# Masks by replaced scores, earlier direct down weights and a split last bank in a hybrid decoder block

## The chip, the cores and the metric

The kernel runs on one core of a Trainium2 chip. The metric is the device time of one execution in microseconds (us), the median of several runs. TensorE (PE) does the matrix products and its weight loads (PEld), VectorE (DVE), ScalarE (ACT) and GpSimd (POOL) the work on elements, SyncE (SP) issues nearly all transfers.

## The reference, cut to what matters

One decoder block on x of 512 x 1024 (float32): an RMS norm, one input projection, a mixture of dilated windows (8 heads), a sparse attention in which an indexer picks at most 128 keys for each query, a gated merge, and a SwiGLU FFN of width 2816 with a final RMS norm. The two pieces that the change touches:

```python
# sparse attention: the 128 best keys of each query
score = jnp.einsum('bqh,bqhs->bqs', wi_blk, jax.nn.relu(dots)) * IDX_SCALE
score = jnp.where(causal[None], score, -jnp.inf)
_, sel = lax.top_k(score, topk)
valid = sel <= q_pos[None, :, None]
...
# the end of the block
x = x + (jax.nn.silu(h @ w_gate) * (h @ w_up)) @ w_down
return rmsnorm(x, norm_final)
```

## The kernel before

All matrices are float32. Each operand of a product is split into a rounded high part and a low rest (`hi`, `lo`), and `mm3` (L202) makes each product with three matmuls. Weights come by SP into `raw` buffers (five), ACT writes `whi`, and DVE or POOL subtracts to get `wlo` (L159 to L175); `PLO` sets which of the two does it. The FFN's down projection is done in two parts: 18 of the 22 blocks of 128 rows through a scheme with seven products instead of eight, the last four (`LAST = 4`) directly.

PE's order over the middle of the program is the order in which the code is traced. The other engines' orders are set by a scheduler that places operations by priority levels: attention at level 2, the filling projections at level 3, the top-k at level 4, so that top-k operations fall between others on DVE. Each engine runs its own list strictly in order. A bank of `acc` (three of them hold the projections), of `tr` (two) or `s` (three) is used again only when its reader is done.

**The top-k** (`topk_ops`, L626). Blocks 3, 2 and 1 of 128 queries have 512, 384 and 256 keys. Sixteen rounds of `max` (the eight largest of a row) and, but for the last round, `match_replace` (those eight are overwritten with `LOWEST` in `cur`) leave 128 values in `top`. Then six operations for each block make the mask: the count of values equal to the 128th (`e0`, L642), the positions equal to it (`eq`, L644), their running count (L646), the equal ones that are still wanted (L647), plus the greater ones (L648), and 0 or -1e30 (L649). Keys after the query hold `LOWEST` from an affine select (L872).

**What stands around it.** While the masks are made, PE runs attention steps of the first mixer (`sc`, `pT`, `y`) between projections: `proj`, four products with 256 columns for the values of the first mixer, block of queries by block; then `slot`, the queries of the second. `va_parts` (L554) empties each `proj` bank by two ACT copies (L564) and two DVE subtractions (L565). `rope_T` (L487) copies a finished `slot` (L490), has SP move its rows crosswise into `sw` (L493), and multiplies and adds on DVE (`straight` L497, `crossed` L500 and L501).

**The end.** With `pair` at its last value, PE makes the remaining products of the seven-product scheme; then DVE adds what these leave to `x1` (ten operations, at L1157, L1159, L1167, L1168 and L1170). The eight direct weights (`W`, L1171) are traced behind these sums: POOL makes the `wlo` of each h = 0, DVE that of each h = 1. Then for each block b of 128 tokens and each half h of 512 columns PE makes 12 matmuls into `po[b, h]`, DVE adds (L1184), ACT squares with a row sum (L1187), POOL multiplies by the norm weights `gF` (L1188), DVE adds up the mean square `v` (L1190). `rstd_of` (L257) is a square root on ACT, a reciprocal and two steps of refinement on DVE (L265 and L269, twice). At last DVE scales h = 0 (L1193), ACT h = 1 (L1195), and SP issues both stores.

Of the kernel before, what the change touches and what calls it, by code (L numbers as in the profile page):

```python
# [11 lines left out]
F32 = mybir.dt.float32  # L12
F32R = mybir.dt.float32r
AF = mybir.ActivationFunctionType
ALU = mybir.AluOpType

P = 128
T = 512
D = 1024
KT = D // P  # L20
NB = T // P
# [3 lines left out]
NF = DFF // P  # L25
D_IN = 4808
TOPK = 128
EPS = 1e-6
NEG = -1.0e30
LOWEST = -3.0e38  # L30
ATTN_SCALE = HD ** -0.5
IDX_SCALE = (64 ** -0.5) * (8 ** -0.5)

# [5 lines left out]
def hybrid_block(ctx: ExitStack, tc: tile.TileContext, x, norm_mix, w_in, w_up_a, w_up_b, w_out,  # L39
                 norm_ffn, w_gate, w_up, w_down, norm_final, c_rope, c_ropeT, c_mask, out):  # L40
    nc = tc.nc
    x2 = x.rearrange("b t d -> (b t) d")
    out2 = out.rearrange("b t d -> (b t) d")
    win, wua, wub, wo = w_in[0], w_up_a[0], w_up_b[0], w_out[0]
    wg, wu, wd = w_gate[0], w_up[0], w_down[0]
# [3 lines left out]
    small = ctx.enter_context(tc.tile_pool(name="small", bufs=4))  # L49
    at_stack = ExitStack()  # L50
    wp = ctx.enter_context(tc.tile_pool(name="wp", bufs=1))
    ap = at_stack.enter_context(tc.tile_pool(name="ap", bufs=1))
# [160 lines left out]
    def trp(name="tr"):  # L213
        return ps.tile([P, 512], F32, tag="tr", bufs=2, name=name)
# [409 lines left out]
    top, cur = {}, {}  # L624

    def topk_ops():  # L626

        for r in range(TOPK // 8):
            for b in (3, 2, 1):
                src = score[b] if r == 0 else cur[b]  # L630
                yield nc.vector.max(top[b][:, 8 * r:8 * r + 8], src[:, :(b + 1) * P])
            if r < TOPK // 8 - 1:
                for b in (3, 2, 1):
                    w = (b + 1) * P
                    src = score[b] if r == 0 else cur[b]
                    yield nc.vector.match_replace(cur[b][:, :w], top[b][:, 8 * r:8 * r + 8], src[:, :w], LOWEST)
        for b in (3, 2, 1):
            w = (b + 1) * P
            thr = top[b][:, TOPK - 1:TOPK]
            need = small.tile([P, 1], F32, name="need")  # L640
            e0 = ap.tile([P, TOPK], F32, tag="e0", bufs=1, name="e0")
            yield nc.vector.tensor_scalar(e0, top[b], thr, None, op0=ALU.is_equal, op1=ALU.add, accum_out=need)  # L642
            eq = ap.tile([P, 512], F32, tag="eq", bufs=1, name="eq")[:, :w]
            yield nc.vector.tensor_scalar(eq, score[b][:, :w], thr, None, op0=ALU.is_equal)  # L644
            cs = cur[b][:, :w]
            yield nc.vector.tensor_tensor_scan(cs, eq, eq, 0.0, op0=ALU.add, op1=ALU.bypass)  # L646
            yield nc.vector.scalar_tensor_tensor(eq, cs, need, eq, op0=ALU.is_le, op1=ALU.mult)  # L647
            yield nc.vector.scalar_tensor_tensor(eq, score[b][:, :w], thr, eq, op0=ALU.is_gt, op1=ALU.add)  # L648
            yield nc.vector.tensor_scalar(score[b][:, :w], eq, 1.0, -NEG, op0=ALU.subtract, op1=ALU.mult)  # L649
            maskb[b] = score[b]  # L650

    topk = []
# [201 lines left out]
    score = {}  # L854
    for b in (3, 2, 1):
        w = (b + 1) * P
        score[b] = sc = ap.tile([P, 512], F32, tag="score", bufs=3, name=f"score{b}")
        sp = k2(name="scorep") if PH[0] >= 0 else None
        for hp in range(4):
            for s, p_ in enumerate(qk_units([(idxT[1 + hp], idxT[0], s, b) for s in range(2)], "dots")):  # L860
                h = 2 * hp + s
                rl = ap.tile([P, 512], F32, tag="sm", bufs=4, name="relu")
                nc.scalar.activation(rl[:, :w], p_[:, :w], AF.Relu)
                eng, to = (nc.gpsimd, sp) if h in PH else (nc.vector, sc)
                if h == 0 or h == PH[0]:
                    eng.tensor_scalar(to[:, :w], rl[:, :w], wis[:, b, h:h + 1], 1.0, op0=ALU.mult, op1=ALU.mult)
                else:
                    eng.scalar_tensor_tensor(to[:, :w], rl[:, :w], wis[:, b, h:h + 1], to[:, :w], op0=ALU.mult, op1=ALU.add)
                if sp is not None and h == NH - 1:
                    nc.vector.tensor_tensor(sc[:, :w], sc[:, :w], sp[:, :w], op=ALU.add)  # L870
            fill(DOTF)
        nc.gpsimd.affine_select(out=sc[:, b * P:w], in_=sc[:, b * P:w], compare_op=ALU.is_ge, fill=LOWEST, base=0,  # L872
                                pattern=[[-1, P]], channel_multiplier=1)
    drain()
    for b in (3, 2, 1):
# [76 lines left out]
    x1 = [load_x(b) for b in range(NB)]  # L952
# [26 lines left out]
    fp = ctx.enter_context(tc.tile_pool(name="fp", bufs=1))  # L979
# [5 lines left out]
    for h in range(2):  # L985
        W = chunk(wo, [(512 * h, 512)], per=1)
        po = [alloc("x1") for alloc in ((sps, sps, sps, trp) if h == 0 else (trp, sps, sps, sps))]
# [13 lines left out]
        for b in range(NB):  # L1001
            jk = k2(name="junk")
# [3 lines left out]
    gF = fp.tile([P, D], F32, name="gF")  # L1006
# [23 lines left out]
    for f in range(0, NF, 2):  # L1030
        G = []
        pair = f // 2
        W = chunk(wg, [(f * P, 256)])
        for j in range(2):
            p_ = acc("g")
            for k in range(KT):
                mm3(p_, (W[k][0][:, j * P:(j + 1) * P], W[k][1][:, j * P:(j + 1) * P]), h2[k], k == 0, k == KT - 1)
            g = fp.tile([P, 512], F32, tag="g", bufs=2, name="g")
# [3 lines left out]
        W = chunk(wu, [(f * P, 256)])  # L1042

        ops = fp.tile([P, 8, 256], F32, tag="ops", bufs=1, name="ops") if pair < NS else None
        for j in range(2):
            p_ = acc("u")
# [10 lines left out]
            tag, bufs = (("y", YB) if i >= 2 else ("rp", 2) if i == 1 else ("k2", K2))  # L1057
# [17 lines left out]
    po = {(b, h): banks[2 * b + h](f"o{b}{h}") for b in range(NB) for h in range(2)}  # L1075
# [19 lines left out]
    def product(b0, h, a, o, w, start, stop):  # L1095

        for i in range(2):
            c = slice(o + i * P, o + (i + 1) * P)
            mm3(po[b0 + i, h], (a[0][:, c], a[1][:, c]), w, start, stop)
# [45 lines left out]
    for pair in range(NS):  # L1145
        bring_back(pair + BACK)
        a, s5 = back[pair]
        w21, w22, u3 = second_weights(pair) if pair else first_of_second
        if pair == NS - 1:
            product(2, 0, a, 256, u3, False, True)  # L1150
        product(0, 0, a, 0, w21, pair == 0, False)
        product(0, 1, s5, 0, w22, pair == 0, False)
        if pair < NS - 1:
            product(2, 0, a, 256, u3, pair == 0, False)
    for i in range(2):
        o = x1[2 + i][1]
        nc.vector.tensor_tensor(o, o, po[2 + i, 0], op=ALU.subtract)  # L1157
        o = x1[2 + i][0]
        nc.vector.tensor_tensor(o, po[2 + i, 0], o, op=ALU.add)  # L1159
# [5 lines left out]
    for i in range(2):  # L1165
        o = x1[2 + i][0]
        nc.vector.tensor_tensor(o, po[2 + i, 1], o, op=ALU.add)  # L1167
        nc.vector.tensor_tensor(o, o, V[i], op=ALU.add)  # L1168
        o = x1[2 + i][1]
        nc.vector.tensor_tensor(o, o, c5[i], op=ALU.add)  # L1170
    W = {}  # L1171
    for f in range(NF - LAST, NF):
        for h in range(2):
            W[f, h] = chunk(wd[f * P:(f + 1) * P], [(512 * h, 512)], kts=1, per=1)[0]
    for i in range(2):
        nc.gpsimd.tensor_scalar(gF[:, i * 512:(i + 1) * 512], gF[:, i * 512:(i + 1) * 512], 0.0625, 1.0, op0=ALU.mult, op1=ALU.mult)
    for b in range(NB):
        v = None
        for h in range(2):
            for f in range(NF - LAST, NF):  # L1180
                mm3(po[b, h], (act[f][0][:, b * P:(b + 1) * P], act[f][1][:, b * P:(b + 1) * P]), W[f, h],
                    b >= 2 and f == NF - LAST, f == NF - 1)
            o = x1[b][h]
            nc.vector.tensor_tensor(o, po[b, h], o, op=ALU.add)  # L1184
            ss = small.tile([P, 1], F32, name="ss3")
            jk = fp.tile([P, 512], F32, tag="g", bufs=2, name="jk")
            nc.scalar.activation(jk, o, AF.Square, accum_out=ss)  # L1187
            nc.gpsimd.tensor_tensor(o, o, gF[:, h * 512:(h + 1) * 512], op=ALU.mult)  # L1188
            v2 = small.tile([P, 1], F32, name="v3")
            nc.vector.tensor_scalar(v2, ss, 1.0 / D, EPS if v is None else v, op0=ALU.mult, op1=ALU.add)  # L1190
            v = v2
        rs3 = rstd_of(v, 1, f"rs3_{b}", scaled=True)
        nc.vector.tensor_scalar(x1[b][0], x1[b][0], rs3, None, op0=ALU.mult)  # L1193
        nc.sync.dma_start(out2[b * P:(b + 1) * P, 0:512], x1[b][0])
        nc.scalar.activation(x1[b][1], x1[b][1], AF.Copy, scale=rs3)  # L1195
        nc.sync.dma_start(out2[b * P:(b + 1) * P, 512:1024], x1[b][1])


def _constants():
# [10 lines left out]
    n[d < 0] = 0  # L1210
    mask = np.where(n > 0, np.log(np.maximum(n, 1)) / ATTN_SCALE, NEG).astype(np.float32)
    return tab, tabT, mask
# [24 lines left out]
```

## Time and profile before

| what | us |
|---|---|
| median of 3 runs | 767.15 |
| lowest and highest run | 764.58, 769.06 |
| the profiled execution | 764.99 |
| its span, first to last instruction | 763.2 |
| PE busy in it | 733.3 |
| DVE, ACT, POOL busy | 503.4, 378.4, 258.8 |

An engine that is busy here is not always what the others wait for: a list of waits tells who waited for whom, a timeline tells when. The timeline gives start, duration, engine, line, output and inputs; in brackets is the idle time just before, and what ended it. Durations of neighbours overlap a little, since an engine takes up the next operation while the last one drains.

### The profile page before, as it was taken

To read this page: it belongs to the slowest core of one execution; us is meant where nothing else is said; L and a number is where in the kernel's file an instruction comes from. 1 tells how busy PE (TensorE), PEld (TensorE's weight loads), DVE (VectorE), ACT (ScalarE), POOL (GpSimd) and SP (SyncE) were. 2 spreads that over 40 slices of the span, in tenths; PEclk is the share of its full clock that TensorE was granted. 3 is DMA by queue.
4 is the path that set the end of the run, shared out by engine and by line. 5 is a ranking of instruction groups with operands and counts; after the bars stand their busy time and mean duration, and the time that the engine had idled before them with its cause. 6 is when DMAs were issued, how large, how long until landed. Compare 5 with 4: busy or idle time off the path is not lost.

```text
span 763.2 us, 10914 instructions
## 1 busy us (share of the span) xinstructions
PE 733.3 (96%) x3567; PEld 616.1 (81%) x3567; DVE 503.4 (66%) x1063; ACT 378.4 (50%) x771; POOL 258.8 (34%) x245
## 2 busy tenths in 40 slices
PE   8987998997999999999999999999999999999995
PEld 7976887886888888888887888888888888888874
DVE  5879998999757557848225444344454457877885
ACT  6366656665656666634246333333333334545553
POOL 1653567563554554523222222222222220000043
PEclk9999999999999999999999999999999999999999
DMA  7342243322342212443332343334433452756722
GB/s 266 96 124 70 67 120 91 95 65 70 84 126 70 69 57 69 141 137 105 100 85 69 103 131 110 104 105 131 131 105 104 130 179 84 230 171 212 248 84 110
DMA packets 76280, 88.70 MB, mean 116 GB/s; under 512 B 6256, under 2 KB 57600, under 8 KB 76224
## 3 DMA queue, kind: packets, MB, share of 16 engines
q1 hardware_dynamic: 76224, 88.02, 38.3%
q8 instruction: 28, 0.46, 0.2%
q14 instruction: 28, 0.23, 0.1%
HBM read 79.08 MB, written 5.64 MB: 111 GB/s over the span
## 4 chain that ended last, share of the span: by engine, by line
PE 79%; DVE 13%; ACT 3%; issue 3%; DMA 1%; POOL 1%; SPq 0%; DVEq 0%; ACTq 0%; POOLq 0%
PE u L204 5%; PE u L205 5%; PE u L203 5%; PE g L205 5%; PE g L204 5%; PE g L203 5%; PE o L205 4%; PE o L203 4%; PE o L204 4%; PE gate L203 3%; PE gate L204 3%; PE gate L205 3%; PE x L203 2%; PE x L205 2%; PE x L204 2%
## 5 line engine op out<-in xcount | busy, mean ns | idle before, releaser
L166 POOL TENSOR_TENSOR wlo<-raw,whi 128x512 fp32r<-128x512 f32 (+1 forms) x138 | 183.4, 1339 | 401.8 <-ACT whi L174 398.5
L174 ACT ACTIVATE whi<-raw 128x512 fp32r<-128x512 f32 (+1 forms) x206 | 126.7, 624 | 164.2 <-PE u L205 70.0
L166 DVE TENSOR_TENSOR wlo<-raw,whi 128x512 fp32r<-128x512 f32 x68 | 50.7, 746 | 67.6 <-ACT whi L174 67.1
L205 PE MATMUL g<-h2l,whi 128*128 128x512 f32 x176 | 68.7, 390 | 0.0
L203 PE MATMUL g<-h2h,whi 128*128 128x512 f32 x176 | 68.7, 390 | 0.0
L204 PE MATMUL g<-h2h,wlo 128*128 128x512 f32 x176 | 68.6, 390 | 0.0
L203 PE MATMUL u<-h2h,whi 128*128 128x512 f32 x176 | 68.5, 389 | 0.0
L204 PE MATMUL u<-h2h,wlo 128*128 128x512 f32 x176 | 68.5, 389 | 0.0
L205 PE MATMUL u<-h2l,whi 128*128 128x512 f32 x176 | 68.5, 389 | 0.0
L686 POOL TENSOR_SCALAR sm<-sm,st 128x256 f32<-128x256 f32 (+3 forms) x64 | 40.0, 632 | 60.1 <-DVE st L685 50.8
L203 PE MATMUL gate<-hTh,whi 128*128 128x512 f32 x128 | 51.6, 403 | 0.0
L205 PE MATMUL gate<-hTl,whi 128*128 128x512 f32 x128 | 50.2, 392 | 0.0
L204 PE MATMUL gate<-hTh,wlo 128*128 128x512 f32 x128 | 50.1, 392 | 0.0
L1050 DVE TENSOR_TENSOR u<-u,rb 128x512 f32<-128x512 f32 x22 | 15.2, 691 | 49.0 <-PE u L205 49.0
L681 ACT ACTIVATE sm<-sm,st 128x256 f32<-128x256 f32 (+3 forms) x64 | 35.6, 557 | 23.6 <-DVE st L680 23.5
L203 PE MATMUL slot<-hTh,whi 128*128 128x512 f32 x104 | 42.4, 407 | 1.8 <-DVE va L565 1.1
L203 PE MATMUL proj<-whi,hTh 128*128 128x256 f32 (+1 forms) x128 | 38.3, 301 | 3.7 <-DVE va L565 1.6
L205 PE MATMUL slot<-hTl,whi 128*128 128x512 f32 x104 | 41.6, 400 | 0.0
L204 PE MATMUL slot<-hTh,wlo 128*128 128x512 f32 x104 | 41.4, 398 | 0.0
L203 PEld LDWEIGHTS u<-h2h,whi 128*128 128x128 f32 x176 | 33.0, 188 | 6.9
L204 PEld LDWEIGHTS u<-h2h,wlo 128*128 128x128 f32 x176 | 33.0, 188 | 6.9
L204 PE MATMUL proj<-whi,hTl 128*128 128x256 f32 (+1 forms) x128 | 38.0, 297 | 0.6 <-DVE hTl L315 0.6
(351 smaller groups left out, 1849.1 us busy)
## 6 DMA issues: line engine op xcount, KB each, us to landing
raw<-in_w_in SPq DMA_DIRECT2D x54, 256.0 KB, 3.0
raw<-in_w_gate SPq DMA_DIRECT2D x44, 256.0 KB, 2.8
raw<-in_w_up SPq DMA_DIRECT2D x44, 256.0 KB, 2.9
raw<-in_w_down SPq DMA_DIRECT2D x43, 256.0 KB, 4.2
wraw<-in_w_down SPq DMA_DIRECT2D x28, 256.0 KB, 3.3
x<-in_x SPq DMA_DIRECT2D x16, 256.0 KB, 4.6
raw<-in_w_in SPq DMA_DIRECT2D x32, 128.0 KB, 2.6
raw<-in_w_out SPq DMA_DIRECT2D x16, 256.0 KB, 2.6
```

The costliest lines, as they stand in the source:

```text
L166: eng.tensor_tensor(lo, raw, hi.bitcast(F32), op=ALU.subtract)
L174: nc.scalar.activation(hi, raw, AF.Copy)
L203: nc.tensor.matmul(o, l[0], r[0], start=start, stop=False)
L204: nc.tensor.matmul(o, l[1], r[0], start=False, stop=False)
L205: nc.tensor.matmul(o, l[0], r[1], start=False, stop=stop)
L681: nc.scalar.activation(sm, sm, AF.Exp, bias=st[:, 0:1], scale=-1.0, accum_out=st[:, 1:2])
L686: nc.gpsimd.tensor_scalar(sm, sm, st[:, 2:3], 1.0, op0=ALU.mult, op1=ALU.mult)
L1050: nc.vector.tensor_tensor(u, p_, rb2, op=ALU.mult)
```

## The change

Four edits. **Masks:** `match_replace` runs in the last round too, so that all 128 chosen scores are `LOWEST` in `cur`, and one operation per block makes the mask: not equal to `LOWEST`, times -1e30. Keys after the query now hold `NEVER` (-3.3e38), another value than `LOWEST`. **Weights:** the loop that makes `W` stands ahead of the ten sums. **Norm weights:** POOL multiplies h = 0 alone; ACT scales h = 0, and DVE multiplies h = 1 by scale and norm weights in one operation. **Last bank:** `po[3, 1]` is made as two halves of 256 columns, the second in a bank of `tr` (`o_end`), each with its own add, square and `v`; the last store of h = 0 is issued by ACT.

```diff
-            if r < TOPK // 8 - 1:
-                for b in (3, 2, 1):
+            for b in (3, 2, 1):
...
-            thr = top[b][:, TOPK - 1:TOPK]
-            need = small.tile([P, 1], F32, name="need")
-            e0 = ap.tile([P, TOPK], F32, tag="e0", bufs=1, name="e0")
-            yield nc.vector.tensor_scalar(e0, top[b], thr, None, op0=ALU.is_equal, op1=ALU.add, accum_out=need)
-            eq = ap.tile([P, 512], F32, tag="eq", bufs=1, name="eq")[:, :w]
-            yield nc.vector.tensor_scalar(eq, score[b][:, :w], thr, None, op0=ALU.is_equal)
-            cs = cur[b][:, :w]
-            yield nc.vector.tensor_tensor_scan(cs, eq, eq, 0.0, op0=ALU.add, op1=ALU.bypass)
-            yield nc.vector.scalar_tensor_tensor(eq, cs, need, eq, op0=ALU.is_le, op1=ALU.mult)
-            yield nc.vector.scalar_tensor_tensor(eq, score[b][:, :w], thr, eq, op0=ALU.is_gt, op1=ALU.add)
-            yield nc.vector.tensor_scalar(score[b][:, :w], eq, 1.0, -NEG, op0=ALU.subtract, op1=ALU.mult)
+            yield nc.vector.tensor_scalar(score[b][:, :w], cur[b][:, :w], LOWEST, NEG, op0=ALU.not_equal, op1=ALU.mult)
...
+    W = {}
+    for f in range(NF - LAST, NF):
+        for h in range(2):
+            W[f, h] = chunk(wd[f * P:(f + 1) * P], [(512 * h, 512)], kts=1, per=1)[0]
     for i in range(2):
         o = x1[2 + i][1]
         nc.vector.tensor_tensor(o, o, po[2 + i, 0], op=ALU.subtract)
...
+            if (b, h) == (NB - 1, 1):
+                parts[b, h] = [(po[b, h], slice(0, 256)), (trp("o_end"), slice(256, 512))]
+            for p_, cs in parts[b, h]:
...
+            if h == 0:
+                nc.gpsimd.tensor_tensor(x1[b][0], x1[b][0], gF[:, 0:512], op=ALU.mult)
         rs3 = rstd_of(v, 1, f"rs3_{b}", scaled=True)
-        nc.vector.tensor_scalar(x1[b][0], x1[b][0], rs3, None, op0=ALU.mult)
-        nc.sync.dma_start(out2[b * P:(b + 1) * P, 0:512], x1[b][0])
-        nc.scalar.activation(x1[b][1], x1[b][1], AF.Copy, scale=rs3)
+        nc.scalar.activation(x1[b][0], x1[b][0], AF.Copy, scale=rs3)
+        (nc.scalar if b == NB - 1 else nc.sync).dma_start(out2[b * P:(b + 1) * P, 0:512], x1[b][0])
+        nc.vector.scalar_tensor_tensor(x1[b][1], x1[b][1], rs3, gF[:, 512:1024], op0=ALU.mult, op1=ALU.mult)
         nc.sync.dma_start(out2[b * P:(b + 1) * P, 512:1024], x1[b][1])
```

DVE's list where the masks are made, before: `va` subtractions empty the banks of `proj`, and `sw`, `z` belong to `rope_T`.

```order
L497 TENSOR_TENSOR z<-raw,ropeT 64x512
L647 SCALAR_TENSOR_TENSOR eq<-cur_1085,need,eq 128x512
L642 TENSOR_SCALAR e_1249,need<-top_1088 128x128
L648 SCALAR_TENSOR_TENSOR eq<-score_738,top_1084,eq 128x512
L649 TENSOR_SCALAR score_738<-eq 128x512
L565 SCALAR_TENSOR_TENSOR va_2081<-proj,rs_147,va_2081 128x2x64
L644 TENSOR_SCALAR eq<-score_838,top_1086 128x384
L500 TENSOR_TENSOR sw<-sw,ropeT 64x512
L565 SCALAR_TENSOR_TENSOR va_2084<-proj,rs_147,va_2084 128x2x64
L501 TENSOR_TENSOR z<-z,sw 64x512
L646 SCALAR_TENSOR_TENSOR cur_1087<-eq 128x384
```

The same place of DVE's list in the changed kernel:

```order
L636 MATCH_REPLACE cur_1087<-top_1086,cur_1087 128x384
L675 RECIPROCAL st<-st 128x1
L636 MATCH_REPLACE cur_1089<-top_1088,cur_1089 128x256
L498 TENSOR_TENSOR z<-raw,ropeT 64x512
L639 TENSOR_SCALAR score_738<-cur_1085 128x512
L639 TENSOR_SCALAR score_838<-cur_1087 128x384
L639 TENSOR_SCALAR score_958<-cur_1089 128x256
L566 SCALAR_TENSOR_TENSOR va_2060<-proj,rs_147,va_2060 128x2x64
L566 SCALAR_TENSOR_TENSOR va_2063<-proj,rs_147,va_2063 128x2x64
L501 TENSOR_TENSOR sw<-sw,ropeT 64x512
L502 TENSOR_TENSOR z<-z,sw 64x512
```

All three masks are now done at one place, and both subtractions of the first `proj` bank stand ahead of the operation on `sw`; before, the masks of 384 and 256 keys stood further down, mixed with the subtractions of the later banks.

DVE's list a little further, before: the first L565 here is the last reader of the second `proj` bank, which PE needs for the `slot` that follows.

```order
L462 TENSOR_TENSOR kBl<-z,kBh 64x512 x2
L685 RECIPROCAL st<-st 128x1 x2
L565 SCALAR_TENSOR_TENSOR va_2084<-proj,rs_147,va_2084 128x2x64
L716 TENSOR_TENSOR A1y<-y,low 64x512
L700 TENSOR_TENSOR ptl<-pT,pth 128x4x128
L700 TENSOR_TENSOR ptl<-pT,pth 128x2x128
```

The same place of DVE's list in the changed kernel:

```order
L463 TENSOR_TENSOR kBl<-z,kBh 64x512 x2
L675 RECIPROCAL st<-st 128x1 x2
L566 SCALAR_TENSOR_TENSOR va_2060<-proj,rs_147,va_2060 128x2x64
L706 TENSOR_TENSOR A1y<-y,low 64x512
L690 TENSOR_TENSOR ptl<-pT,pth 128x4x128
L690 TENSOR_TENSOR ptl<-pT,pth 128x2x128
L566 SCALAR_TENSOR_TENSOR va_2063<-proj,rs_147,va_2063 128x2x64
```

The last reader of that bank is now va_2063, and it has moved behind the two operations on `ptl`.

DVE's list at the end, before: `wlo` are the splits of the direct weights of h = 1, the rest are the ten sums.

```order
L166 TENSOR_TENSOR wlo<-raw,whi 128x512 x2
L1157 TENSOR_TENSOR x_1_3987<-x_1_3987,o_6537 128x512
L1159 TENSOR_TENSOR x_0_3985<-o_6537,x_0_3985 128x512
L1157 TENSOR_TENSOR x_1_3991<-x_1_3991,o_6539 128x512
L1159 TENSOR_TENSOR x_0_3989<-o_6539,x_0_3989 128x512
L1167 TENSOR_TENSOR x_0_3985<-o_6538,x_0_3985 128x512
L1170 TENSOR_TENSOR x_1_3987<-x_1_3987,c_0_7045 128x512
L1168 TENSOR_TENSOR x_0_3985<-x_0_3985,V_7047 128x512
L1167 TENSOR_TENSOR x_0_3989<-o_6540,x_0_3989 128x512
L1170 TENSOR_TENSOR x_1_3991<-x_1_3991,c_1_7046 128x512
L1168 TENSOR_TENSOR x_0_3989<-x_0_3989,V_7048 128x512
L166 TENSOR_TENSOR wlo<-raw,whi 128x512 x2
```

The same place of DVE's list in the changed kernel:

```order
L167 TENSOR_TENSOR wlo<-raw,whi 128x512 x2
L1151 TENSOR_TENSOR x_1_3966<-x_1_3966,o_6516 128x512
L1153 TENSOR_TENSOR x_0_3964<-o_6516,x_0_3964 128x512
L167 TENSOR_TENSOR wlo<-raw,whi 128x512
L1151 TENSOR_TENSOR x_1_3970<-x_1_3970,o_6518 128x512
L1153 TENSOR_TENSOR x_0_3968<-o_6518,x_0_3968 128x512
L1161 TENSOR_TENSOR x_0_3964<-o_6517,x_0_3964 128x512
L167 TENSOR_TENSOR wlo<-raw,whi 128x512
L1162 TENSOR_TENSOR x_0_3964<-x_0_3964,V_7026 128x512
L1164 TENSOR_TENSOR x_1_3966<-x_1_3966,c_0_7024 128x512
L1161 TENSOR_TENSOR x_0_3968<-o_6519,x_0_3968 128x512
L1164 TENSOR_TENSOR x_1_3970<-x_1_3970,c_1_7025 128x512
```

The third split has moved ahead of eight of the sums and the fourth ahead of five. The lists of SP, POOL and ACT stand as before here, but for the operations of the last lines themselves.

## Rows read from the trace of the kernel before

**Rows 1.** The page's chain of work that ended last, by engine.

```profile
PE 79%; DVE 13%; ACT 3%; issue 3%; DMA 1%; POOL 1%; SPq 0%; DVEq 0%; ACTq 0%; POOLq 0%
```

**Rows 2.** Busy us in one stretch: PE, PEld, DVE, ACT, POOL, clock, DMA.

```profile
155.00:200.00 45.00, 39.80 (x235) 34.30 (x234) 39.90 (x97) 25.22 (x62) 23.48 (x23) 1.00 0.31 81
```

**Rows 3.** What PE waited for, 155 to 200: us, times, longest.

```profile
PE sc L615 <- DVE st L680: 1.4, 1, 1.4
PE y L710 <- DVE st L685: 1.2, 1, 1.2
PE slot L203 <- DVE va L565: 1.1, 1, 1.1
PE proj L203 <- DVE va L565: 0.9, 1, 0.9
```

**Rows 4.** Mask operations on DVE: busy by tile (eq, e), then min/median/max ns.

```profile
160.00:190.00 30.00, 14.33 (x15) 1.00 0.32 84
160.00:190.00 30.00, 1.01 (x6) 1.00 0.32 84
L636 DVE MATCH_REPLACE8 cur<-top,cur x42: 400/542/681, 79.7 to 162.2; 128x512 f32<-128x512 f32 x14, 128x384 f32<-128x384 f32 x14, 128x256 f32<-128x256 f32 x14
L649 DVE TENSOR_SCALAR score<-eq x3: 360/428/1264, 171.9 to 186.4; 128x512 f32<-128x512 f32 x1, 128x384 f32<-128x384 f32 x1, 128x256 f32<-128x256 f32 x1
```

**Rows 5.** DVE's timeline in the stage of the masks.

```profile
172.80 0.67 DVE L500 TENSOR_TENSOR sw<-sw,ropeT 64x512 f32<-64x512 f32 x1
177.60 0.33 DVE L565 SCALAR_TENSOR_TENSOR va<-proj,rs,va 128x128 fp32r<-128x128 f32 x1
178.63 1.02 DVE L700 TENSOR_TENSOR ptl<-pT,pth 128x512 fp32r<-128x512 f32 x2
```

**Rows 6.** The transfers into sw: SP's issue, and their landings.

```profile
167.86 1.15 SPq L493 DMA_DIRECT2D sw<-raw  x2
DMA to landing us min/median/max: 2.0/2.1/3.4
```

**Rows 7.** Timeline where the direct weights are split.

```profile
733.01 1.30 POOL L166 TENSOR_TENSOR wlo<-raw,whi 128x512 fp32r<-128x512 f32 x1 [1.12 <-ACT whi L174]
737.19 1.28 DVE L166 TENSOR_TENSOR wlo<-raw,whi 128x512 fp32r<-128x512 f32 x2
737.92 0.50 PE L205 MATMUL o<-wlo,a20h 128*128 128x512 f32 x1 [1.10 <-DVE wlo L166]
```

**Rows 8.** Timeline of the end, after PE's last matmul.

```profile
755.49 0.69 DVE L1184 TENSOR_TENSOR x<-o,x 128x512 f32<-128x512 f32 x1 [0.29 <-PE o L205]
756.28 0.63 ACT L1187 ACTIVATE jk<-x 128x512 f32<-128x512 f32 x1 [1.26 <-DVE x L1184]
757.08 1.26 POOL L1188 TENSOR_TENSOR x<-x,gF 128x512 f32<-128x512 f32 x1 [0.71 <-ACT jk L1187]
757.71 0.64 DVE L265 SCALAR_TENSOR_TENSOR rs_t<-rs,v 128x1 f32<-128x1 f32 x1
759.10 0.49 DVE L1193 TENSOR_SCALAR x<-x,rs 128x512 f32<-128x512 f32 x1
```

**Rows 9.** All eight runs of line 265: min/median/max ns.

```profile
L265 DVE SCALAR_TENSOR_TENSOR rs_t<-rs,v x8: 219/219/667, 742.7 to 758.6; 128x1 f32<-128x1 f32 x8
```

**Rows 10.** Timeline rows of operations with 256 columns, PE, ACT, DVE.

```profile
161.02 0.28 PE L204 MATMUL proj<-whi,hTl 128*128 128x256 f32 x1
161.14 0.28 PE L205 MATMUL proj<-wlo,hTh 128*128 128x256 f32 x1
715.88 0.40 ACT L1026 ACTIVATE s5h<-rb 128x256 fp32r<-128x256 f32 x1
716.96 0.42 DVE L1027 TENSOR_TENSOR s5l<-rb,s5h 128x256 fp32r<-128x256 f32 x1
```

**Rows 11.** GB/s of all transfers, 754 to 764 in slices of 0.25.

```profile
GB/s 0 0 0 0 0 344 360 402 385 393 213 0 0 0 0 0 0 0 0 0 0 0 0 0 0 66 377 385 385 385 393 107 0 0 0 0 0 0 0 0
```

**Rows 12.** Another stretch: PE busy us, granted clock, DMA share, GB/s.

```profile
130.00:135.00 5.00, 3.14 (x8) 0.69 0.20 52
```

More of the change, by code (lines that the diff above doesn't have):

```diff
@@ L30 @@
 LOWEST = -3.0e38
+NEVER = -3.3e38
 ATTN_SCALE = HD ** -0.5
@@ L631, in topk_ops @@
                 yield nc.vector.max(top[b][:, 8 * r:8 * r + 8], src[:, :(b + 1) * P])
-            if r < TOPK // 8 - 1:
-                for b in (3, 2, 1):
-                    w = (b + 1) * P
-                    src = score[b] if r == 0 else cur[b]
-                    yield nc.vector.match_replace(cur[b][:, :w], top[b][:, 8 * r:8 * r + 8], src[:, :w], LOWEST)
+            for b in (3, 2, 1):
+                w = (b + 1) * P
+                src = score[b] if r == 0 else cur[b]
+                yield nc.vector.match_replace(cur[b][:, :w], top[b][:, 8 * r:8 * r + 8], src[:, :w], LOWEST)
         for b in (3, 2, 1):
             w = (b + 1) * P
-            thr = top[b][:, TOPK - 1:TOPK]
-            need = small.tile([P, 1], F32, name="need")
-            e0 = ap.tile([P, TOPK], F32, tag="e0", bufs=1, name="e0")
-            yield nc.vector.tensor_scalar(e0, top[b], thr, None, op0=ALU.is_equal, op1=ALU.add, accum_out=need)
-            eq = ap.tile([P, 512], F32, tag="eq", bufs=1, name="eq")[:, :w]
-            yield nc.vector.tensor_scalar(eq, score[b][:, :w], thr, None, op0=ALU.is_equal)
-            cs = cur[b][:, :w]
-            yield nc.vector.tensor_tensor_scan(cs, eq, eq, 0.0, op0=ALU.add, op1=ALU.bypass)
-            yield nc.vector.scalar_tensor_tensor(eq, cs, need, eq, op0=ALU.is_le, op1=ALU.mult)
-            yield nc.vector.scalar_tensor_tensor(eq, score[b][:, :w], thr, eq, op0=ALU.is_gt, op1=ALU.add)
-            yield nc.vector.tensor_scalar(score[b][:, :w], eq, 1.0, -NEG, op0=ALU.subtract, op1=ALU.mult)
+            yield nc.vector.tensor_scalar(score[b][:, :w], cur[b][:, :w], LOWEST, NEG, op0=ALU.not_equal, op1=ALU.mult)
             maskb[b] = score[b]
@@ L871, in hybrid_block @@
             fill(DOTF)
-        nc.gpsimd.affine_select(out=sc[:, b * P:w], in_=sc[:, b * P:w], compare_op=ALU.is_ge, fill=LOWEST, base=0,
+        nc.gpsimd.affine_select(out=sc[:, b * P:w], in_=sc[:, b * P:w], compare_op=ALU.is_ge, fill=NEVER, base=0,
                                 pattern=[[-1, P]], channel_multiplier=1)
@@ L1170, in hybrid_block @@
         nc.vector.tensor_tensor(o, o, c5[i], op=ALU.add)
[L1171 to L1174, printed above, removed]
     for i in range(2):
         nc.gpsimd.tensor_scalar(gF[:, i * 512:(i + 1) * 512], gF[:, i * 512:(i + 1) * 512], 0.0625, 1.0, op0=ALU.mult, op1=ALU.mult)
+    parts = {(b, h): [(po[b, h], slice(0, 512))] for b in range(NB) for h in range(2)}
     for b in range(NB):
@@ L1179, in hybrid_block @@
         for h in range(2):
[L1180 to L1191, printed above, removed]
+            if (b, h) == (NB - 1, 1):
+                parts[b, h] = [(po[b, h], slice(0, 256)), (trp("o_end"), slice(256, 512))]
+            for p_, cs in parts[b, h]:
+                for f in range(NF - LAST, NF):
+                    mm3(p_[:, cs], (act[f][0][:, b * P:(b + 1) * P], act[f][1][:, b * P:(b + 1) * P]), [w[:, cs] for w in W[f, h]],
+                        b >= 2 and f == NF - LAST, f == NF - 1)
+                o = x1[b][h][:, cs]
+                nc.vector.tensor_tensor(o, p_[:, cs], o, op=ALU.add)
+                ss = small.tile([P, 1], F32, name="ss3")
+                jk = fp.tile([P, 512], F32, tag="g", bufs=2, name="jk")
+                nc.scalar.activation(jk[:, cs], o, AF.Square, accum_out=ss)
+                v2 = small.tile([P, 1], F32, name="v3")
+                nc.vector.tensor_scalar(v2, ss, 1.0 / D, EPS if v is None else v, op0=ALU.mult, op1=ALU.add)
+                v = v2
```

## The prediction, made blind

> **What bounds the kernel now.** I read the page's chain first: PE holds 79% of the chain that ended last and DVE 13% [rows 1]. So an edit to DVE's work counts only where PE waits for it, and behind PE's last matmul. Then I read the stages and the list of PE's waits. Between 155 and 200 us PE is busy for 39.80 of 45 us, and DVE for 39.90 [rows 2]; four of PE's waits there end with an operation of DVE: 0.9 us for the `va` subtraction that frees a bank for `proj`, 1.1 us for the one that frees a bank for `slot`, 1.4 us before `sc`, 1.2 us before `y`, together 4.6 us [rows 3]. The reader should see that this is just where DVE makes the masks. At the end there are two more places: PE idles 1.10 us for a split weight [rows 7], and after PE's last matmul a chain DVE, ACT, DVE runs alone [rows 8].
>
> **Masks.** Removed are fifteen operations on `eq`, 14.33 us, and those on `e0`, 1.01 us [rows 4]: 15.3 us of DVE. Added are three `match_replace`, 542 ns in the median [rows 4], 1.6 us, and three `tensor_scalar` of the form of L649, 428 ns in the median [rows 4], 1.3 us. DVE loses about 12.4 us where it had almost no idle time. What of that reaches PE goes by the four waits.
>
> The first, 0.9 us: about a third of the 15.3 us stood ahead of the two subtractions that free this bank, the mask of 512 keys; the six operations that now do all three masks take 2.9 us in all. I take this wait as gone; its price has one answer.
>
> The second, 1.1 us, is the one that decides. The bank for `slot` is freed by the subtraction which ran at 177.60, and PE started at 178.08. In the new list that subtraction stands behind the two operations on `ptl`, which ran at 178.63 for 1.02 us [rows 5]. They hang on a chain through ACT that begins with `z`, that is with L500, and L500 waits for `sw`. The two transfers were issued from 167.86 for 1.15 us and land 2.1 us after their issue [rows 6], so near 170.7; with the copy ahead of them some 0.8 us sooner, near 169.9. L500, at 172.80 before [rows 5], can start near 170.4 with its wait and what is left ahead of it: 2.4 us sooner. The two operations on `ptl` then end at 178.63 + 1.02 - 2.4 = 177.25, the subtraction follows with 0.33 us [rows 5], and `slot` starts near 177.6 instead of 178.08. Of the first two waits together PE therefore gains only 0.5 us; it reaches `slot` 0.9 us sooner, near 176.1, and stands there in one piece for 1.5 us or more. Bounds: 0, if L500 moves less than 2 us, and 2.0, if the chain keeps up altogether.
>
> The third and fourth, 1.4 and 1.2 us, end with the softmax of DVE that stood behind two whole masks. Nothing but five subtractions stands ahead of it now. I take both as gone: 2.6 us; bounds 0, if another engine ends last there, and 2.6. The later stages run on PE, so what is gained here stays. Masks: 0.5 + 2.6 = 3.1 us, between 0.5 and 4.6.
>
> **A port that DVE and POOL share** speaks against the new mask operations. L649 took 360 ns at its fastest and 1264 ns at its slowest [rows 4]. L265, one column wide, took 219 ns in the median and 667 at worst [rows 9]; in the last block it began at 757.71 and lasted 0.64 us, while POOL's L1188 ran from 757.08 for 1.26 us [rows 8]: both end within 0.02 us of each other. So an operation of DVE can stand until POOL's is over. The Trainium skill, "SBUF — State Buffer", section "Who interferes with whom", says that a two-port operation of DVE, or one with two SBUF inputs, and an operation of POOL exclude each other for a whole instruction; by that rule the trace agrees, and each of the new operations could lose that time.
>
> **Weights.** The 1.10 us [rows 7] fall away: the third split stands eight sums sooner and the fourth five; five sums of about 0.6 us (estimated from L1184's 0.69 [rows 8], since neighbours overlap) put the fourth 3 us ahead of the 737.19 at which it began. Next late is POOL's split of the last weight of h = 0: it ran at 733.01 for 1.30 us [rows 7], to 734.31. PE runs 76 matmuls from 737.92 to the add at 755.49, 0.23 us each [rows 7, 8], and needs this one nine matmuls ahead of the one that waited from 736.82, so near 734.75: 0.4 us to spare. If it slips by as much as one more operation of DVE with the port, 0.5 us come back. Weights: 1.1 us, between 0.6 and 1.1. The sums that now run later free nothing that PE wants soon; they end before the add of block 0, which PE doesn't wait for.
>
> **The end.** Matmuls with 256 columns start 0.12 us apart [rows 10]: 24 of them take 2.88 us where twelve of 0.23 took 2.76, so +0.12. The last add falls from 0.69 [rows 8] to about 0.42, the square from 0.63 to about 0.40 [rows 8, 10]: -0.27 and -0.23. The add, square and `v` of the first half fit under the second half's 1.44 us. POOL no longer works while L265 runs, since its share is over one bank earlier: 0.64 becomes 0.22 [rows 8, 9], -0.42. Against that, the first store had left after L1193's 0.49 us; the fused operation has two tensors and is priced like the add, 0.69 [rows 8]: +0.20. This counts in full, because the two stores fill the transfer engines without a gap at about 385 GB/s [rows 11]: the end moves with the first of them. For the same reason the store from ACT's queue gains nothing; no row has such an issue, so it costs between 0 and 1.3 us, the spread of landings in [rows 6], and I take 0, since the rate is the bound. The Trainium skill, "Trainium Kernel Development and Optimization", section "Key Constraints", says likewise that queues of several engines share the same transfer engines and save only issue time; by that nothing is gained here either. The end: 0.12 - 0.27 - 0.23 - 0.42 + 0.20 = -0.6 us, between -1.2 (the fused operation as fast as L1193, and 0.4 less in the chain) and +0.7.
>
> **Sum.** 3.1 + 1.1 + 0.6 = 4.8 us. The profiled execution took 764.99 us, which gives 760.2; it lies 2.2 us below the median of the runs, 767.15, and the same gain from that gives 762.3. I forecast medians: 762.3 us, a ratio of 0.994.
>
> **The rivals.** First, *the slot wait goes too*. For it: L500's transfer may have landed earlier, and ACT is busy for only 25.22 of 45 us [rows 2]. Then the masks give 4.6, the sum is 6.3: 760.85.
>
> Second, *the port takes it back*: each of the three new mask operations meets one of POOL's and takes 1.26 instead of 0.43 us [rows 4], 2.5 us more, of which some 1 us hides under the landing of `sw`. For it: POOL is busy for 23.48 of the 45 us [rows 2]; against it: the median of the three L649 is near the fastest [rows 4]. The slot starts 1.5 us later than forecast, the sum is 3.3: 763.85. The Trainium skill's rule named above would bring it about.
>
> Third, *the waits change their names*: `sc` and `y` wait for ACT or POOL instead, since the step's softmax needs all three engines and POOL has a queue of weight splits there. The 2.6 us stay, the sum is 2.2: 764.95.
>
> Fourth, the other side, *the clock*. In 130 to 135 PE was busy for only 3.14 of 5 us and the granted clock showed 0.69, part of it at the level of 1.2 GHz [rows 12]; from 155 to 200 it was 1.00 throughout, at 2.4 GHz, in spite of the waits [rows 2]. The wait before `slot`, now 1.5 us or more in one piece, could bring it down. A fall as in that row costs 0.31 of 5 us, 1.6 us, and leaves a gain. It decides from 4.8 us of loss on, 9.6 us at the lower level; over the 12 us from `slot` to `y` it would cost 6: 768.35, slower than before.
>
> **How the numbers follow.** Forecast 56%, the first rival 12%, the second 13%, the third 15%, the fourth 4%. A median of runs that spread from 764.58 to 769.06 wanders by 1 to 2 us. The range 759.0 to 765.5 reaches from below the first rival to above the third and leaves out the fourth and the tails. About 0.5%, 3.8 us, is what a measurement here can tell from no change: below 763.3 counts as faster. Most of the forecast and nearly all of the first rival lie there, a third of the second and little of the third: faster 0.65. The rest of these within the bound: 0.30. Slower: the fourth and a bad draw, 0.05.
>
> **What would show it.** In the changed profile DVE is about 12 us less busy. PE's list of waits between 155 and 200 should have no `proj` and no `sc` or `y` behind DVE, but one wait of about 1.5 us before `slot`; if that row is missing, the first rival holds, if it has 3 us, the second. PE should go from the seven-product scheme to the direct products without a wait for `wlo`. L265 should last 0.22 us in all blocks, and from the last add to the last scaling some 2.7 us should pass where 3.6 did. The prediction is wrong if new waits of PE appear after 190 us, or the clock shows less than 1.00 there.

## The result, and the profile after

| | us | ratio to the kernel before |
|---|---|---|
| before, median of 8 runs | 766.28 (761.39 to 769.06) | |
| changed kernel, median of 8 runs | 771.34 (767.84 to 773.24) | 1.0063, 95% interval 1.0039 to 1.0086 |
| its profiled execution, and its span | 770.18, 768.4 | |

The change made the kernel slower by 0.6%, where 762.3 us was forecast. The first row of the page after already says where to look: DVE is 10 us less busy, where about 12 were forecast, but PE, on which the end hangs, is busy for 744.7 us instead of 733.3. It has 12 matmuls more on record, and those (256 columns, two for one) explain 0.1 us.

```profile
PE 744.7 (97%) x3579; PEld 617.6 (80%) x3579; DVE 493.5 (64%) x1053; ACT 379.4 (49%) x773; POOL 251.0 (33%) x241
```

The edits themselves did what they say. In the stage of the masks, the list of PE's waits for 155 to 200 us, which had four rows behind DVE in [rows 3], has one row left in the changed kernel (us in all, times, longest); two short waits of `pT`, 0.3 and 0.2 us, which [rows 3] leaves out, are gone too:

```profile
PE slot L204 <- DVE va L566: 2.7, 1, 2.7
```

The busy time of each engine in stretches (us of the stretch, then PE, PEld, DVE, ACT, POOL, clock, DMA) shows it too: PE 42.35 of 45 us where it had 39.80, DVE 33.11 where it had 39.90 [rows 2]. The second row is a stretch of the FFN, where PE does nothing but products of 512 columns:

```profile
155.00:200.00 45.00, 42.35 (x247) 37.18 (x246) 33.11 (x88) 27.02 (x65) 22.30 (x23) 0.96 0.35 91
420.00:620.00 200.00, 200.00 (x863) 162.13 (x862) 88.02 (x147) 68.34 (x108) 46.54 (x36) 1.00 0.37 115
```

The same stretch in the kernel before:

```profile
420.00:620.00 200.00, 200.00 (x884) 165.66 (x883) 90.04 (x149) 68.71 (x109) 46.67 (x36) 1.00 0.39 122
```

Both have PE busy without a gap at a clock of 1.00, and the changed kernel gets 863 matmuls done where the kernel before got 884 (recorded ones). No edit touches this code. Three matmuls in a row from PE's timeline (start, duration, engine, line, operation, output and inputs), before (lines 203 to 205) and then changed (lines 204 to 206), show that it is neither a wait nor an idle time: none has a bracket, and the starts lie 0.22 or 0.23 us apart before, 0.23 and now and then 0.24 in the changed kernel.

```profile
500.02 0.39 PE L205 MATMUL g<-h2l,whi 128*128 128x512 f32 x1
500.25 0.39 PE L203 MATMUL g<-h2h,whi 128*128 128x512 f32 x1
500.47 0.39 PE L204 MATMUL g<-h2h,wlo 128*128 128x512 f32 x1
```

```profile
500.03 0.39 PE L205 MATMUL g<-h2h,wlo 128*128 128x512 f32 x1
500.26 0.40 PE L206 MATMUL g<-h2l,whi 128*128 128x512 f32 x1
500.49 0.41 PE L204 MATMUL g<-h2h,whi 128*128 128x512 f32 x1
```

Over a stretch this adds up. I call **spacing** the mean distance between the starts of neighbouring matmuls of 512 columns, from the starts in 420 to 620 us: 226.7 ns before, 232.4 ns after. The groups of instructions by line say the same, 389 and 395 ns in the mean for one matmul (before, then changed):

```profile
L203 PE MATMUL g<-h2h,whi 128*128 128x512 f32 x144 | 56.0, 389 | 0.0
```

```profile
L204 PE MATMUL g<-h2h,whi 128*128 128x512 f32 x144 | 56.8, 395 | 0.0
```

To see where the time went I cut both profiled executions at the same matmuls of PE's timeline, since PE's list is the same in both but at the very end. The fourth and fifth columns are two of the experiments below.

| stretch, us | before | after | e1 | e2 |
|---|---|---|---|---|
| start to the first `proj` of the masks' stage | 160.91 | 158.48 | 158.54 | 157.97 |
| from there to the first `gate` behind it | 34.94 | 33.12 | 33.16 | 34.96 |
| to the first `g` | 208.38 | 211.38 | 208.38 | 211.42 |
| to the last `u` | 241.99 | 247.87 | 241.95 | 247.86 |
| to PE's last matmul | 108.85 | 110.21 | 109.61 | 112.31 |
| to the end of the span | 8.09 | 7.34 | 7.65 | 8.09 |

In the second and the last row the edits gain 1.8 and 0.8 us. In the third and fourth, where nothing was edited, the changed kernel loses 3.0 and 5.9 us. The `g` and `u` products are 6 groups of 176 matmuls, 1056 in all; at 5.7 ns more for each that is 6.0 us, the loss of that row. (The first row differs by 2 to 3 us between executions whose lists are alike there, e2 and before among them. The fifth row has some of the loss too: about 330 of its matmuls are of the slow kind that the next section describes, 1.9 us at 5.7 ns each; and its waits of PE come to 1.1, 0.2, 1.1 and 2.0 us in the four executions.)

### The profile page after: what moved, and what is told of

Same layout as the page of the kernel before. It is cut to its first block, busy times and chain, and to the rows that moved or that the text cites. A ratio compares the mean times of both kernels' runs of the same rounds, so it can differ in the third digit from the quotient of the medians.

```text
span 768.4 us, 10923 instructions
## 1 busy us (share of the span) xinstructions
PE 744.7 (97%) x3579; PEld 617.6 (80%) x3579; DVE 493.5 (64%) x1053; ACT 379.4 (49%) x773; POOL 251.0 (33%) x241
## 4 chain that ended last, share of the span: by engine, by line
PE 74%; DVE 7%; ACT 2%; issue 1%; DMA 0%; SPq 0%; ACTq 0%; DVEq 0%
PE u L205 5%; PE u L204 5%; PE u L206 5%; PE g L205 5%; PE g L206 5%; PE g L204 5%; PE o L204 4%; PE o L205 4%; PE o L206 4%; PE gate L204 3%; PE gate L205 3%; PE gate L206 3%; PE x L206 2%; PE x L204 2%; PE x L205 2%; PE up L204 2%
## 5 line engine op out<-in xcount | busy, mean ns | idle before, releaser
L206 PEld LDWEIGHTS u<-h2l,whi 128*128 128x128 f32 x176 | 33.2, 188 | 7.7
```

## The theories

What changed for these matmuls, if not their list? The masks no longer need the tile `need`, four buffers of one value for each partition, padded to 32 bytes each, in the pool `small`. The pools lie in SBUF one behind the other: `kp` (the column operands `hT`, `h2`, `y`, the first `a` and those of the last products), then `small`, then `wp` (`raw`, `whi`, `wlo`), then `fp` (the `a` of the middle of the seven-product scheme). With `need` gone, everything behind `small` lies 128 bytes lower in the program's allocation: the first `whi` at 124000 instead of 124128. `kp` stays where it was, at 20448. All these tiles are a multiple of 2048 bytes long, so that every `whi` and `wlo` has one and the same distance to every column tile in `kp`, modulo 256: 0 before, 128 after.

**Theory A:** the matmul gets slower since the weights' address relative to the columns' address has changed. The trace of the changed kernel holds a control. In 670 to 700 us PE runs the seven-product scheme with `a` from `fp`, which moved together with `whi`; there the spacing is 226.7 ns and as many matmuls stand in the row of before as of after, 134 (stretch, PE of tile `o`, PEld, DVE, ACT, clock; before, then changed):

```profile
670.00:700.00 30.00, 30.00 (x134) 24.84 (x133) 1.28 (x2) 2.26 (x4) 1.00 0.56 179
```

```profile
670.00:700.00 30.00, 30.00 (x134) 24.83 (x133) 0.00 (x0) 2.26 (x4) 1.00 0.57 186
```

**Rivals:** the edits themselves slow PE (its queue, or traffic of DVE and POOL at the same time); or the address of the weights by itself counts (an alignment), not the distance. A third would be that the other engines, which write `raw`, `whi` and `wlo` at the moved addresses, get in the way of PE's reads. The changed kernel's trace speaks against it: of the 860 distances between starts in 420 to 620 us, the 173 during which DVE, ACT and POOL did nothing have a mean of 232.2 ns and the others 232.4; the 48 without any transfer either have 232.5.

## The experiments

In all but e4 and e5, unused buffers of the small tile `ss3` put 32 bytes each between `kp` and the weights. Where only that differs, the lists of all engines stay the same, instruction for instruction.

**e1, the changed kernel with the weights moved back by 128 bytes.**

```diff
-                ss = small.tile([P, 1], F32, name="ss3")
+                ss = small.tile([P, 1], F32, name="ss3", bufs=8)
```

> The changed kernel, instruction for instruction, but the row sums ss3 have eight buffers instead of four, which moves everything allocated behind them (raw, whi, wlo, the attention's and the FFN's tiles) up by 128 bytes, back to where whi stood in the kernel before. Theory A (the change also removed the four buffers of need, and whi moved by 128 bytes against hT and h2; matmuls that read one as weights and the other as columns start 232 instead of 227 ns apart): spacing back at 227 ns, and 760 to 764 us, about 4 to 5 us under the kernel before. Theory B (the changed order itself makes PE slower, because the engine idles less or for another reason of the schedule): spacing stays at 232 ns and the time at 771 us.

Measured: 761.98 us (760.28 to 764.06) beside 765.98, ratio 0.9955 (0.9938 to 0.9972). PE busy 733.0 us, spacing 226.7 ns, and the row of the stretch has its 884 matmuls again:

```profile
420.00:620.00 200.00, 200.00 (x884) 165.74 (x883) 91.66 (x151) 70.67 (x112) 47.96 (x37) 1.00 0.38 120
```

So the edits are not what slows PE, and with the addresses as they were the change is worth 4.0 us. This version beats both kernels.

**e2, the kernel before with the weights moved away by 128 bytes.** The same line, in the kernel before.

```diff
-            ss = small.tile([P, 1], F32, name="ss3")
+            ss = small.tile([P, 1], F32, name="ss3", bufs=8)
```

> The kernel before, instruction for instruction, with ss3 in eight buffers: whi and all behind it move up by 128 bytes, so that whi stands against hT and h2 as in the changed kernel, modulo 256. Theory A: matmul spacing 232 ns in the FFN and about 776 us, 10 us over the kernel before. Theory B: 227 ns and 766 us.

Measured: 775.81 us (774.43 to 778.09), ratio 1.0140 (1.0109 to 1.0172); spacing 232.4 ns.

```profile
420.00:620.00 200.00, 200.00 (x862) 162.13 (x862) 87.63 (x146) 68.34 (x108) 46.55 (x36) 1.00 0.37 116
```

The loss comes and goes with 128 bytes alone, in either kernel: 9.4 us from e1 to the changed kernel, 9.8 from before to e2. The theory stands, and the first rival falls.

**e3, the new masks alone**, with the weights kept at their address.

```diff
-            need = small.tile([P, 1], F32, name="need")
...
+            yield nc.vector.tensor_scalar(score[b][:, :w], cur[b][:, :w], LOWEST, NEG, op0=ALU.not_equal, op1=ALU.mult)
...
+            ss = small.tile([P, 1], F32, name="ss3", bufs=8)
```

> The kernel before with the new masks alone, and ss3 in eight buffers so that whi keeps its address. By the prediction's step on the masks 3.1 us less than the kernel before, 763 us, with one wait of PE before slot of 1.5 us or more and none behind DVE for proj, sc and y. Theory A: spacing 227 ns. Theory B, were the masks its cause: 232 ns and 774 us.

Measured: 763.37 us (761.75 to 768.48), ratio 0.9960 (0.9942 to 0.9979): 2.6 us gained by the medians. The profiled execution is the longest of its 14, 768.48 us. From the first `proj` to `gate` it takes 33.15 us, like e1. At the end its profile has waits that the edits on weights and end would have touched, and one before the last half of the seven-product scheme (`V`) that comes with 0 to 2.9 us in the executions shown here.

```profile
PE o L204 <- DVE V L1134: 2.9, 1, 2.9
PE o L206 <- DVE wlo L167: 1.3, 1, 1.3
```

**e4, weights, norm weights and last bank alone** (the masks as before, so that `need` and all addresses stay).

```diff
+    W = {}
+    for f in range(NF - LAST, NF):
...
+                parts[b, h] = [(po[b, h], slice(0, 256)), (trp("o_end"), slice(256, 512))]
...
+        nc.vector.scalar_tensor_tensor(x1[b][1], x1[b][1], rs3, gF[:, 512:1024], op0=ALU.mult, op1=ALU.mult)
```

> The kernel before with the new end alone (direct weights ahead of the sums, norm weights and scale in one operation, last bank in two). Addresses of whi, hT and h2 are those of the kernel before. By the prediction's steps on weights and end 1.7 us less, 764.6 us. Theory A: spacing 227 ns. Theory B, were the end its cause: more than 766 us.

Measured: 764.74 us (762.51 to 769.26), ratio 0.9996 (0.9975 to 1.0016). By the medians 1.2 us are gained; by the interval that cannot be told from nothing, so the end edits' gain by itself is not shown by the times. e3 and e4 together give 3.8 us, e1 with all of it 4.0.

**e5, weights and columns moved together.** Four unused buffers in the first pool move all that lies behind it by 128 bytes: `whi` to 124128, where it is fast in the kernel before, and `kp` to 20576.

```diff
-    warm = const.tile([P, 1], F32, name="warm")
+    warm = const.tile([P, 1], F32, name="warm", bufs=5)
```

> The changed kernel, instruction for instruction, with four unused slots of 32 bytes more in the first pool. Everything that lies behind that pool moves up by 128 bytes: the weights whi and wlo to exactly the addresses that they have in the kernel before, and the column tiles (hT, h2, y, a) with them, so that the distance between weights and columns stays what it is in the changed kernel. Theory A (the distance decides): matmuls of 512 columns stay 232 ns apart, PE busy near 745 us, time near 771 us. Rival B (the address of the weights by itself decides): 226.7 ns, PE busy near 733, time near 762 as in the run where the weights alone were moved by 128 bytes.

Measured: 770.55 us (768.05 to 772.79), ratio 1.0052 (1.0026 to 1.0079); PE busy 745.2 us, spacing 232.4 ns.

```profile
420.00:620.00 200.00, 200.00 (x862) 162.25 (x862) 87.54 (x146) 68.42 (x110) 46.54 (x36) 1.00 0.37 115
```

As slow as the changed kernel, with the weights at the very address that is fast in the kernel before. The second rival falls: the distance counts, not the address.

**e6 to e12, the distance in steps of 32 bytes.** All are the changed kernel with another number of buffers in e1's line (6, 12, 5, 7, 9, 10, 11 in the order of their numbers).

```diff
-                ss = small.tile([P, 1], F32, name="ss3")
+                ss = small.tile([P, 1], F32, name="ss3", bufs=6)
```

> The changed kernel, instruction for instruction, with the weights moved up by 64 bytes against the columns (halfway between the slow distance, 128 modulo 256, and the fast one, 0). Graded theory: the cost falls with the distance from the slow place, spacing near 229.5 ns and PE busy near 739 us. Step theory: only the place at 128 is slow, 226.7 ns and PE busy near 733 us, time near 762.

> The changed kernel, instruction for instruction, with the weights moved up by 256 bytes against the columns. If the dependence repeats every 256 bytes (the distance is again 128 modulo 256): 232 ns, PE busy near 745 us, time near 771. If it repeats only at 512 or more, or if any distance but the one of the changed kernel is fast: 226.7 ns, 733 us, near 762.

> The changed kernel, instruction for instruction, with the weights moved up by 32 bytes against the columns (160 modulo 256). Graded theory: near 231 ns, PE busy near 742 us. Step theory: 226.7 ns and 733 us, if the slow place is narrower than 32 bytes; 232 ns and 745 us, if it is wider.

> The changed kernel, instruction for instruction, with the weights moved up by 96 bytes against the columns (distance 224 modulo 256). Measured so far per matmul: 226.7 ns at 0, 232.3 at 128, 233.4 at 160, 228.9 at 192. Theory of a graded conflict with its best place at 0: between 226.7 and 228.9 ns, PE busy 733 to 739 us, time 762 to 766. Theory that the best place lies below 0: less than 226.7 ns (the fall from 160 to 192 is 4.5 ns in 32 bytes), and a time below 762.

> The changed kernel, instruction for instruction, with the weights moved up by 160 bytes (distance 32 modulo 256). If the best place is 0: between 226.7 and 232.3 ns, near 228 by a straight line from 0 to 128, time near 763.5. If the best place lies above 0: less than 226.7 ns and a time below 762.

> The changed kernel, instruction for instruction, with the weights moved up by 192 bytes (distance 64 modulo 256). If the dependence were symmetric about 0, it would be that of 192: 228.9 ns, PE busy 739 us, near 766. If it rises in a straight line from 0 to 160: 229.4 ns, near 766. If the best place lies above 0: less than 226.7 ns.

> The changed kernel, instruction for instruction, with the weights moved up by 224 bytes (distance 96 modulo 256). By a straight line from 0 to 160: 230.7 ns, PE busy near 742 us, time near 768. If the slow region is narrow and begins only near 128: 226.7 ns and 762.

All of them, by the distance of the weights from `kp` modulo 256:

| distance | run | spacing, ns | PE busy, us | time, us (runs) |
|---|---|---|---|---|
| 0 | before | 226.7 | 733.3 | 766.28 (8) |
| 0 | e1 | 226.7 | 733.0 | 761.98 (12) |
| 32 | e10 | 233.3 | 746.4 | 772.13 (9) |
| 64 | e11 | 233.3 | 746.5 | 771.11 (10) |
| 96 | e12 | 234.3 | 749.2 | 775.39 (4) |
| 128 | changed kernel | 232.4 | 744.7 | 771.34 (8) |
| 128 | e7 | 232.4 | 745.3 | 771.42 (1) |
| 160 | e8 | 233.3 | 748.7 | 774.70 (1) |
| 192 | e6 | 228.9 | 739.2 | 766.33 (1) |
| 224 | e9 | 233.3 | 745.6 | 772.72 (5) |

e7 is as slow as the changed kernel at 256 bytes more, so the dependence repeats there; that it repeats everywhere was not tried. The graded theory came within 0.6 ns in e6 alone; e8 to e12 came out against it, and so did the two forecasts of 226.7 ns in e8 and e12: 192 is nearly fast (228.9), 224, though nearer to 0, is slow, and 64 is not the mirror of 192. Of eight distances one is fast, one nearly so, and six cost 5.7 to 7.6 ns more for each matmul. The kernel before stood on the fast one, and none beats it. The control from above holds in every run: with columns from `fp`, which move with the weights, the spacing in 670 to 700 us is 226.7 to 227.5 ns in e5 to e12, so that none of the eight places of the weights modulo 256 is slow by itself. What happens inside PE at the other distances stays open: no run shows it.

The Trainium skill, "SBUF — State Buffer", section "Who interferes with whom", gives PE two read ports, one for the columns and one for weight loads, calls them independent, and says that PE never waits on anyone. Read so, the distance should not matter; here it changes the pace of the same list by 5.7 ns for each matmul, and the measurement decides.

## Why the prediction was wrong, point by point

**The step that failed** is one that the sum never took. Each edit was costed by its instructions and waits, and the matmuls were carried over at the "0.23 us each" of the kernel before; the sentence "The later stages run on PE, so what is gained here stays" rests on that. The prediction counted the operations that fall away and did not ask what becomes of the tile `need`, nor what lies behind it in SBUF. The changed kernel's matmuls take 5.7 ns more wherever the weights meet columns from `kp`, 9.4 us in all. No rival had it, and the signs that were named (new waits of PE after 190 us, a clock below 1.00 there) could not show it: PE doesn't wait, and the clock is 1.00.

With the addresses kept, the forecast's number would have held: 762.3 us, and e1 took 761.98. Part of that is luck: the forecast took 4.8 us from a median of 767.15 over three runs, while e1 gained 4.0 on a median of 765.98 over 29. The terms were of unequal quality, too.

**Masks, 3.1 us: the mechanism right, the size 1.3 us too large in the two traces** (34.94 to 33.12 us, 1.8; by the medians e3 gained 2.6, 0.5 less than forecast). The part up to `slot` came out as worked: its first matmul was put at 177.6, 16.7 us behind the first `proj`, and it started at 175.20, 16.7 us behind 158.48. The operations that decide, from DVE's timeline, to be read beside [rows 5]:

```profile
168.36 0.67 DVE L501 TENSOR_TENSOR sw<-sw,ropeT 64x512 f32<-64x512 f32 x1
173.77 1.02 DVE L690 TENSOR_TENSOR ptl<-pT,pth 128x512 fp32r<-128x512 f32 x2
174.71 0.60 DVE L566 SCALAR_TENSOR_TENSOR va<-proj,rs,va 128x128 fp32r<-128x128 f32 x2
```

The operation on `sw` stands 9.9 us behind the first `proj` where it stood 11.9 us behind it: 2.0 us sooner, 2.4 were forecast. The wait before `slot` is 2.65 us, "1.5 us or more" as said, since PE got there sooner than I had it; the rival that it goes too is out. The waits of `sc` and `y` are gone and none took their place here (e1 and e3 have 0.7 us before `pT`), so the third rival is out. But their 2.6 us, and the 0.5 of `pT`, did not all arrive: from `slot` to `gate` PE took 16.4 us instead of 17.8, 1.4 us less. The fourth rival's mechanism accounts for the rest. Stretches of 5 us in the changed kernel (PE busy, clock, DMA share, GB/s), the level of 1.2 GHz part of the time in the middle one:

```profile
170.00:175.00 5.00, 2.55 (x22) 1.00 0.01 3
175.00:180.00 5.00, 4.80 (x17) 0.66 0.40 98
180.00:185.00 5.00, 5.00 (x23) 1.00 0.39 111
```

PE stood still for 2.65 us, and behind it the granted clock showed 0.66; the `slot` matmuls start 0.42 us apart there. At 0.34 of 4.80 us this is 1.6 us, the very price that the prediction had worked out from [rows 12], but as a rival of 4% and not as a term. All eleven profiled executions with the new masks have such a wait, of 2.7 to 3.3 us, and a fall of the clock behind it. The kernel before showed 1.00 throughout [rows 2], and so did e2. But e4, with the old masks, fell too: behind its waits of 1.4 us before `sc` and 1.1 before `y`, the granted clock shows 0.70, and from the first `proj` to `gate` it took 36.53 us instead of 34.94 (the same view of e4):

```profile
190.00:195.00 5.00, 5.00 (x22) 0.70 0.51 132
```

So the fall is not the price of the merged wait alone: against such an execution the new masks gain 3.4 us, and the 2.6 by the medians lies between 1.8 and 3.4. In e3 and e4 the clock fell likewise behind the waits of 2.9 and 2.5 us before `V` (0.66 in 700 to 705 us). How often the kernel before falls there was not measured, and that the waits bring the clock down is read from these rows and was not tried by itself.

The `slot` matmuls of the changed kernel, behind the wait:

```profile
175.20 0.62 PE L204 MATMUL slot<-hTh,whi 128*128 128x512 f32 x1 [2.65 <-DVE va L566]
175.62 0.63 PE L205 MATMUL slot<-hTh,wlo 128*128 128x512 f32 x1
```

**The port** took one of the three new operations, not all: minimum, median and maximum of the three are 277, 343 and 1494 ns in the changed kernel, and about the same in e1. The first, on 512 keys, ran from 165.43 to 166.93 beside a split on POOL; that the one held the other is read from this overlap. The three were done by 167.40, ahead of the operation on `sw` at 168.36, on which the subtraction that frees the bank hangs through ACT and `ptl`, and `slot` started when it was forecast; so I read no loss to PE from it. The prediction's own sign (a row of 3 us before `slot` for the second rival) would have misled here: 2.65 us is near that, but PE came early and the bank was not late.

```profile
165.07 1.58 POOL L167 TENSOR_TENSOR wlo<-raw,whi 128x512 fp32r<-128x512 f32 x1
165.43 1.97 DVE L639 TENSOR_SCALAR score<-cur 128x512 f32<-128x512 f32 x3
```

```profile
L639 DVE TENSOR_SCALAR score<-cur x3: 277/343/1494, 165.4 to 167.1; 128x512 f32<-128x512 f32 x1, 128x384 f32<-128x384 f32 x1, 128x256 f32<-128x256 f32 x1
```

**Weights, 1.1 us: right in kind.** With the old order PE waited for a `wlo` of DVE 1.1 us [rows 7], 1.7 in e2 and 1.3 in e3. In all eleven executions with the new order that row is gone. What comes late next is POOL's split, as said, in e1 for the 0.5 us that the prediction had named, in the changed kernel not at all. (The prediction gave 737.19 as the start of the fourth split; it is that of the third and fourth, which share a row in [rows 7], and PE waited for the third. That one stands eight sums sooner, so the term is not hurt.) PE's waits behind 640 us, changed kernel, then e1:

```profile
PE o L204 <- DVE V L1134: 0.2, 1, 0.2
```

```profile
PE o L204 <- DVE V L1134: 0.6, 1, 0.6
PE o L206 <- POOL wlo L167: 0.5, 1, 0.5
```

**The end, 0.6 us: right in the trace.** From the last add to DVE's scaling 2.64 us pass (761.37 to 764.01), where 2.7 were forecast and 3.61 had passed [rows 8].

```profile
761.37 0.42 DVE L1179 TENSOR_TENSOR x<-o_end,x 128x256 f32<-128x256 f32 x1
761.89 0.42 ACT L1182 ACTIVATE jk<-x 128x256 f32<-128x256 f32 x1 [0.88 <-DVE x L1179]
763.11 0.22 DVE L266 SCALAR_TENSOR_TENSOR rs_t<-rs,v 128x1 f32<-128x1 f32 x1
764.01 0.75 DVE L1191 SCALAR_TENSOR_TENSOR x<-x,rs,gF 128x512 f32<-128x512 f32 x1
764.82 0.37 ACTq L1190 DMA_DIRECT2D out<-x  x1
```

L266 lost its 0.42 us: all eight took 0.22 us in the changed kernel, where the last block has no POOL operation beside them, and the first of the last block had taken 0.64 [rows 8].

```profile
L266 DVE SCALAR_TENSOR_TENSOR rs_t<-rs,v x8: 218/219/220, 748.1 to 763.6; 128x1 f32<-128x1 f32 x8
```

The fused operation took 0.75 us, 0.06 more than the add that priced it. The stores fill the transfer engines as before [rows 11], so I still take it that ACT's queue gains nothing; no run has both stores on SP. From the start of PE's last matmul to the end of the span it is 7.34 us instead of 8.09, 0.8 less. The eleven executions with the new end have 7.33 to 7.94 us, the three with the old 8.09. The rates of all transfers in 756.4 to 768.4 us, in slices of 0.3:

```profile
GB/s 369 144 0 0 0 0 0 0 0 0 0 0 0 137 355 417 362 403 75 0 0 0 0 0 0 0 0 0 0 0 75 396 369 403 355 150 0 0 0 0
```

## What to carry to other kernels

An edit that adds or removes a tile moves every tile allocated behind it, and a matmul's pace can hang on where its weights lie against its columns; so compare the addresses of the operands before and after, and keep them with a few unused bytes if they moved. When a change makes PE busier without more matmuls, compare the number of matmuls in one stretch without waits at the same clock before looking for a wait. And when short waits of PE merge into one, or go, look at the granted clock behind them in several executions of both kernels: here it fell behind the merged wait each time, and behind the short ones in one execution of three, so that one pair of traces did not give the gain.

## What the runs showed of the hardware that I had not expected

With float32 operands of 512 columns in a rounded form, matmuls started 226.7 ns apart when weights and columns lay a multiple of 256 bytes apart, 228.9 at 192 modulo 256, and 232.4 to 234.3 at the six other multiples of 32 bytes: 1.0% to 3.4% more, in a kernel whose end hangs on PE, and without an idle time, a wait or a lower clock in the trace. The weight loads show nothing of it, 188 ns in the mean before and after:

```profile
L203 PEld LDWEIGHTS g<-h2h,whi 128*128 128x128 f32 x144 | 27.0, 188 | 5.7
```

```profile
L204 PEld LDWEIGHTS g<-h2h,whi 128*128 128x128 f32 x144 | 27.1, 188 | 6.4
```
